# Moving a 32-byte tile from below the weight slots to above them, in a hybrid decoder layer

## The chip, the cores and the metric

The kernel runs on one core of a Trainium2 chip. The metric is the device time of one execution in microseconds (us). A core has five engines that run side by side and meet at semaphores: TensorE (PE in the profile; its weight loads are listed apart as PEld), VectorE (DVE), ScalarE (ACT), GpSimd (POOL) and SyncE (SP), which here only issues DMAs. Tiles lie in the on-chip memory SBUF, 128 partitions wide; an address below is a byte offset inside each partition.

## The reference, cut to what matters

```python
h = rms_norm(x, mix_norm)                       # x: 1024 tokens x 1024
z = h @ w_in                                    # columns: GLA q,k,v,r, low rank | SWA q,k,v
o_gla = gla_chunked(...)                        # gated linear attention, 4 heads, then rms norm and SiLU gate
o_swa = swa_sink_attention(...)                 # window 128, 8 query heads, 2 key heads, ALiBi, sinks
x = x + concat([o_gla, o_swa]) @ w_out
h2 = rms_norm(x, ffn_norm)
u = causal_dwconv(h2 @ w_up, conv_w, conv_b)    # 1024 x 5632, three taps
a, b = split(u, 2)
return x + (silu(a) * b) @ w_down               # 2816 x 1024
```

Everything is float32 and there is one layer.

## The kernel before, in words

Each large product is made in float32r from a high and a low part of both factors (`split`, L88 to L95: `hi` is a rounded copy, `lo` the rest), in three matmuls: high x high, high x low, low x high (`PASSES`). A matmul has a stationary operand (128 x 128, `lhsT`) and a moving one (`rhs`, mostly 128 x 512), and every one has its own weight load.

- Tokens are tiles of 128. The input projections (`dense`, L317, and `unit_q_part`, L707) run over eight token tiles and eight row blocks: `lhsT` is a piece of the normalized, transposed input in `big`, `rhs` a weight block. PSUM names are `dq`, `dk`, `dv`, `dg`, `dr` for the parts of `z` and `do` for the output projection. `dk` has 272 columns, the others 512.
- Between them run the two attentions, with small matmuls and transposes.
- The up-projection (`product`, L834) uses Strassen's seven products for each of 22 chunks of columns: `lhsT` is a weight block (`A11`, `A12`, `A22` or a sum `S1` to `S4` of blocks), `rhs` four token tiles at once, 128 x 4 x 128, from `big` or from `ex` (sums of token blocks). Each product is 12 matmuls. PSUM names are `gb` for most of chunk 0 and `fb` for the others; `fb` also serves the last rows.
- The down-projection (`down_pair`, L1015) uses seven products for each pair of chunks, 10 pairs, in groups of six matmuls that stand between the up products: `lhsT` is `dg` (activations), `rhs` is `dw` (weights), PSUM `dn_P`. The last two chunks are done in `last_row` (L1044, PSUM `dl` and `fb`) from `dnw` and `g`.

Order of the work: the first part is pinned in a list (`FIRST`); after it each step has a due time (`at`, `at_us`) and the program is written out in the order of those times.

Memory: pools on the left grow up from the bottom, pools with `side="right"` grow down from the top. The first pool on the right is `wa` (`w_keep`), nine slots of 2 x 512 floats, 4096 bytes each. `slot_tile` hands out slots, `w_tile` walks through them by `SLOTS`. They hold all the split weights of the projections but seven blocks of `dk`, the up operands, both operands of the down products and the raw rows of `w_down`. Under it lies `idp` with `ident` (512 bytes, the identity for transposes) and `mhalf` (8 floats, 32 bytes), filled with -0.5 and read by GpSimd as the exponent in `rms_scale` and `norm1_stat`. `idp` is closed by `open_ff`, before the tiles of the convolution are opened there. The addresses of the program before:

| tile | address | remainder by 64 |
|---|---|---|
| `big` (activations, high and low) | 1152 | 0; all pieces are 512 bytes apart |
| raw tiles, `kw` (seven blocks of `dk`), `ex` (token sums) | 67392 and on, 160320, 112448 | 0 |
| `A11w` and `A12w` of chunk 1, in the pool `pn` | 178240, 182336 | 0 |
| `w9`, one late slot: block 0 of the second half of `w_out` | 187840 | 0 |
| `ident` | 191936 | 0 |
| `mhalf` | 192448 | 0 |
| nine slots | 192480 + 4096 s, s = 0 to 8 | 32 |
| end of the usable memory | 229344 | 32 |

```python
    w_keep = ctx.enter_context(tc.tile_pool(name="wa", bufs=1, side="right"))
    idp = swp.enter_context(tc.tile_pool(name="idp", bufs=1, side="right"))
    def slot_tile(slot, name, dt=F32R):
        return w_keep.tile([P, 2, 512], dt, tag=f"w{slot}", name=name, bufs=1)
    # product (L834): w from a slot, or from pn for A11 and A12 of chunk 1
    pe.matmul(pb, lhsT=w[:, ra, k, :], rhs=b_operand(bn, k, rb), ...)
    # dense (L317): ws[k] from a slot, from kw or w9
    pe.matmul(pb[:, :n], lhsT=big[:, t, k, ra, :], rhs=ws[k][:, rb, :n], ...)
    # down_pair (L1015): both from slots
    pe.matmul(pb[:, i], lhsT=g[:, ra, c:c + P], rhs=w[:, rb, :], ...)
```

Of the kernel before, what the change touches and what calls it, by code (L numbers as in the profile page):

```python
# [9 lines left out]
F32 = mybir.dt.float32  # L10
# [7 lines left out]
P = 128  # L18
# [16 lines left out]
def hymba_layer_kernel(ctx, tc, x, mix_norm, w_in, w_alpha2, b_alpha, gla_norm,  # L35
# [33 lines left out]
    def raw_tile(name):  # L69
        return base.tile([P, 1024], F32, tag="raw", name=name, bufs=RAW_BUFS)  # L70

    w_keep = ctx.enter_context(tc.tile_pool(name="wa", bufs=1, side="right"))
    w_late = {}
    swp = ExitStack()
    idp = swp.enter_context(tc.tile_pool(name="idp", bufs=1, side="right"))
# [39 lines left out]
    upper = gl.tile([P, P], F32, name="upper")  # L115
    amask = upper.bitcast(I32)
    ind = gl.tile([P, 2], F32R, name="ind")
    mhalf = idp.tile([P, 8], F32, name="mhalf")
    pool.memset(mhalf, -0.5)

    ones_r = gl.tile([P, P], F32R, name="ones_r")
# [1182 lines left out]
```

## Time and profile before

| | |
|---|---|
| median of 3 runs | 1054.98 us (1054.74 to 1055.16) |
| profiled execution, span from first to last instruction | 1053.6 us |
| median less span | 1.4 us |
| matmuls, busy time of TensorE | 4976, 1046.6 us |
| weight loads | 4976, 851.0 us |
| VectorE, ScalarE, GpSimd busy | 799.4, 480.2, 617.7 us |
| DMA moved | 67.13 MB, mean 64 GB/s |

The page gives of the profiled execution its span; the time around it is not listed there, so the median is set against the span. Busy times of TensorE add up overlapping, pipelined matmuls, with modelled ends; how fast it goes is read from the starts of successive matmuls. In the chain that ended last each row is a stretch: start in us, length in us, what ran, and how many instructions.

### The profile page before, as it was taken

The numbers are of one execution on the slowest core, as the hardware profiler recorded it, in microseconds if no ns is written. First come the engines' busy times: TensorE is split into PE (matmuls) and PEld (weight loads), VectorE is DVE, ScalarE is ACT, GpSimd is POOL, SyncE is SP. The second block draws the span as 40 slices with busy tenths as digits, with TensorE's granted clock in tenths as the row PEclk, the third lists the DMA queues.
The fourth block names the chain that finished last, engine by engine and source line by source line (L and its number), as shares of the span: only waits on it lengthen the run. The fifth ranks groups of instructions, "written<-read, shape, count | busy, mean of one in ns | idle before, by whom it ended". The sixth has DMA issues, their size and how long they took to land.

```text
span 1053.6 us, 13921 instructions
## 1 busy us (share of the span) xinstructions
PE 1046.6 (99%) x4976; PEld 851.0 (81%) x4976; DVE 799.4 (76%) x1332; ACT 480.2 (46%) x988; POOL 617.7 (59%) x510
## 2 busy tenths in 40 slices
PE   9999999999999999999999999999999999999998
PEld 6898877888888888888888888888888888888887
DVE  6776667754131699887979898897979798897976
ACT  5527655444340346554444445444444444444441
POOL 4592132325450205867868687877778687978750
PEclk9999999999999999999999999999999999999999
DMA  6152113002044202112121111212121211121104
GB/s 213 61 152 61 44 49 92 21 1 81 1 122 159 60 1 80 40 41 81 40 80 34 49 51 49 60 61 61 40 80 40 61 40 45 56 61 60 41 20 160
DMA packets 67502, 67.13 MB, mean 64 GB/s; under 512 B 4648, under 2 KB 52201, under 8 KB 67434
## 3 DMA queue, kind: packets, MB, share of 16 engines
q1 hardware_dynamic: 63448, 61.27, 18.7%
q10 hardware_dynamic: 3986, 4.99, 2.0%
q8 instruction: 39, 0.64, 0.2%
q14 instruction: 29, 0.24, 0.1%
HBM read 57.33 MB, written 4.19 MB: 58 GB/s over the span
## 4 chain that ended last, share of the span: by engine, by line
PE 97%; DMA 1%; DVE 1%; ACT 0%; issue 0%; POOL 0%; DVEq 0%; ACTq 0%; SPq 0%
PE fb L834 39%; PE dn_P L1015 18%; PE do L317 9%; PE dr L317 4%; PE dv L317 4%; PE dg L317 4%; PE dq L317 3%; PE dk L317 2%; PE gb L834 2%; PE dq L707 1%; PE pv L490 1%; PE dl L1044 1%; PE fb L1044 1%; PE go L600 1%; PE ga L591 1%; PE sc L443 1%
## 5 line engine op out<-in xcount | busy, mean ns | idle before, releaser
L1019 DVE TENSOR_TENSOR acc<-acc,dn_P 128x1024 f32<-128x1024 f32 x140 | 169.8, 1214 | 65.6 <-PE dn_P L1015 65.5
L1015 PE MATMUL dn_P<-dw,dg 128*128 128x512 f32 x840 | 215.8, 392 | 0.0
L1015 PEld LDWEIGHTS dn_P<-dw,dg 128*128 128x128 f32 x840 | 157.7, 188 | 37.1
L317 PE MATMUL do<-wow,big 128*128 128x512 f32 x384 | 92.9, 398 | 0.0
L317 PEld LDWEIGHTS do<-wow,big 128*128 128x128 f32 x384 | 71.1, 188 | 16.3
L95 POOL TENSOR_TENSOR dw<-dn,dw 128x512 fp32r<-128x512 f32 x50 | 69.1, 1381 | 25.3 <-PE dn_P L1015 19.5
L886 ACT COPY ca<-fb 128x512 f32<-128x512 f32 x62 | 36.3, 585 | 72.8 <-PE fb L834 72.7
L834 PE MATMUL fb<-big,A11w 128*128 128x512 f32 x252 | 63.0, 396 | 0.0
L834 PE MATMUL fb<-big,S4w 128*128 128x512 f32 x252 | 62.9, 396 | 0.0
L834 PE MATMUL fb<-big,S1w 128*128 128x512 f32 x252 | 62.9, 396 | 0.0
L834 PE MATMUL fb<-ex,S2w 128*128 128x512 f32 x252 | 62.8, 396 | 0.0
L834 PE MATMUL fb<-ex,S3w 128*128 128x512 f32 x252 | 62.8, 396 | 0.0
L841 DVE SCALAR_TENSOR_TENSOR ua<-fb,cc,ua 128x511 f32<-128x511 f32 x84 | 62.2, 740 | 0.5 <-ACT ua L846 0.3
L834 PE MATMUL fb<-big,A12w 128*128 128x512 f32 x252 | 62.5, 396 | 0.0
L834 PE MATMUL fb<-ex,A22w 128*128 128x512 f32 x252 | 62.5, 397 | 0.0
L834 PEld LDWEIGHTS fb<-big,A11w 128*128 128x128 f32 x252 | 47.4, 188 | 11.6
L834 PEld LDWEIGHTS fb<-big,S1w 128*128 128x128 f32 x252 | 47.4, 188 | 11.6
L834 PEld LDWEIGHTS fb<-big,S4w 128*128 128x128 f32 x252 | 47.4, 188 | 11.6
L834 PEld LDWEIGHTS fb<-ex,S2w 128*128 128x128 f32 x252 | 47.4, 188 | 11.4
L834 PEld LDWEIGHTS fb<-ex,A22w 128*128 128x128 f32 x252 | 47.4, 188 | 11.4
L834 PEld LDWEIGHTS fb<-ex,S3w 128*128 128x128 f32 x252 | 47.4, 188 | 11.4
L834 PEld LDWEIGHTS fb<-big,A12w 128*128 128x128 f32 x252 | 47.3, 188 | 11.1
(432 smaller groups left out, 2402.7 us busy)
## 6 DMA issues: line engine op xcount, KB each, us to landing
up<-in_w_up_dram SPq DMA_DIRECT2D x44, 512.0 KB, 3.9
dn<-in_w_down_dram SPq DMA_DIRECT2D x22, 512.0 KB, 3.5
acc<-in_x_dram SPq DMA_DIRECT2D x8, 512.0 KB, 6.9
out_dram<-acc SPq DMA_DIRECT2D x15, 256.0 KB, 2.0
xt<-in_x_dram SPq DMA_DIRECT2D x7, 512.0 KB, 3.4
vraw<-in_w_in_dram SPq DMA_DIRECT2D x4, 512.0 KB, 3.7
graw<-in_w_in_dram SPq DMA_DIRECT2D x4, 512.0 KB, 3.6
qt<-qt ACTq DMA_DIRECT2D x16, 128.0 KB, 2.2
```

The lines of the kernel that those rows point to most:

```text
L95: (eng or pool).tensor_sub(lo, src, hi.bitcast(F32))
L317: pe.matmul(pb[:, :n], lhsT=big[:, t, k, ra, :], rhs=ws[k][:, rb, :n], start=(k == 0 and i == 0), stop=(k == KD - 1 and i == 2))
L443: pe.matmul(pbs[-1][:, j % 2, :], lhsT=ql[:, g, qc], rhs=kt[:, g, kc], start=False, stop=True)
L490: pe.matmul(pbs[i][HALF[g]], lhsT=vv[rows, t - 1 + b, HALF[g]], rhs=rhs[rows, :, HALF[i]], start=start, stop=stop)
L591: pe.matmul(pb[:, pr * 256:(pr + 1) * 256], lhsT=gqt[t][:, pr, :], rhs=qbd[t % 2][:, pr], start=(pr == 0), stop=(pr == 1))
L600: pe.matmul(pb[:, h * P:(h + 1) * P], lhsT=asb[:, h, :], rhs=v[:, h * P:(h + 1) * P], start=(h == 0), stop=(t == 0 and h == 3))
L834: pe.matmul(pb, lhsT=w[:, ra, k, :], rhs=b_operand(bn, k, rb), start=(onto is None and i == 0), stop=(i == 11), skip_group_check=onto is n ...
L841: dve.scalar_tensor_tensor(dst, src, w, dst, op0=ALU.mult, op1=ALU.add)
L886: act.copy(dst, pb)
L1015: pe.matmul(pb[:, i], lhsT=g[:, ra, c:c + P], rhs=w[:, rb, :], start=(onto is None and n == 0), stop=(n == 2), skip_group_check=onto is no ...
L1019: dve.tensor_add(acc, acc, pb)
L1044: pe.matmul(pb[:, c0:c1], lhsT=g[:, ra, (t % 4) * P:(t % 4 + 1) * P], rhs=w[:, rb, c0:c1], start=(ch == NCH - 2 and i == 0), stop=(ch == N ...
```

## The change

`mhalf` gets a pool of its own, `edge`, which is opened first on the right side and stays open to the end. It lies at 229312, the slots begin at 192448 + 4096 s, 32 bytes lower, where `mhalf` was, and `ident` and everything below it keep their addresses. All nine slots then begin at multiples of 64.

```diff
@@ -69,6 +69,8 @@
     def raw_tile(name):
         return base.tile([P, 1024], F32, tag="raw", name=name, bufs=RAW_BUFS)
 
+    edge = ctx.enter_context(tc.tile_pool(name="edge", bufs=1, side="right"))
+    mhalf = edge.tile([P, 8], F32, name="mhalf")
     w_keep = ctx.enter_context(tc.tile_pool(name="wa", bufs=1, side="right"))
     w_late = {}
     swp = ExitStack()
@@ -115,7 +117,6 @@
     upper = gl.tile([P, P], F32, name="upper")
     amask = upper.bitcast(I32)
     ind = gl.tile([P, 2], F32R, name="ind")
-    mhalf = idp.tile([P, 8], F32, name="mhalf")
     pool.memset(mhalf, -0.5)
 
     ones_r = gl.tile([P, P], F32R, name="ones_r")
```

## The prediction

> **What bounds the kernel now.** I read the page first: busy times, slices, the chain that ended last.
>
> ```profile
> span 1053.6 us, 13921 instructions
> PE 1046.6 (99%) x4976; PEld 851.0 (81%) x4976; DVE 799.4 (76%) x1332; ACT 480.2 (46%) x988; POOL 617.7 (59%) x510
> PEclk9999999999999999999999999999999999999999
> PE 97%; DMA 1%; DVE 1%; ACT 0%; issue 0%; POOL 0%; DVEq 0%; ACTq 0%; SPq 0%
> ```
>
> TensorE is busy nearly always, at the full granted clock, and 97% of the chain is its own matmuls one behind another. The list of what TensorE waited for (engine, line, releaser: us in total, times, longest) is as short as this:
>
> ```profile
> PE warm L1085 <- DVE warm L124: 1.7, 1, 1.7
> PE dg L317 <- ACT vg L720: 0.9, 1, 0.9
> PE dq L707 <- POOL qw L295: 0.3, 1, 0.3
> PE gb L834 <- ACT big L255: 0.2, 1, 0.2
> PE dq L707 <- DVE big L259: 0.2, 1, 0.2
> ```
>
> 3.3 us in all. So the time is set by the distance from one matmul's start to the next, times the count, and nothing else is worth much. A matmul's listed duration does not show that distance, since matmuls overlap (392 ns listed, for one every 230). The chain in order of time does: start, us, what, and how many. The sum by line of the whole chain, then the stretch in which the up-projection begins, then three other stretches:
>
> ```profile
> by line: PE fb L834 39.2%; PE dn_P L1015 18.4%; PE do L317 8.5%; PE dr L317 4.3%; PE dv L317 3.7%; PE dg L317 3.7%; PE dq L317 2.7%; PE dk L317 2.3%; PE gb L834 1.9%; PE dq L707 1.3%; PE pv L490 1.2%; PE dl L1044 1.0%; PE fb L1044 1.0%; PE
> ...
> 312.97 47.83 PE do L317 x205
> 390.38 6.75 PE do L317 x29
> ...
> 403.14 2.81 PE gb L834 x12
> 405.95 2.30 PE fb L834 x10
> ...
> 410.29 2.75 PE fb L834 x12
> ...
> 441.11 14.06 PE fb L834 x60
> ...
> 464.01 1.36 PE dn_P L1015 x6
> ...
> 468.19 1.39 PE dn_P L1015 x6
> ...
> 1036.46 2.72 PE fb L1044 x12
> ```
>
> Divide, and set each beside the addresses in the map above. All these matmuls have the same shape, 128x128 stationary against 512 moving columns:
> - Rows of `do` (L317): 47.83 / 205 = 233.3 ns. Moving operand in a slot (32 past a multiple of 64), stationary in `big` (a multiple of 64).
> - Up products: 14.06 / 60 = 234.3, 2.81 / 12 = 234.2. Stationary in a slot, moving in `big` or `ex`. Again one of each kind.
> - The last rows (L1044): 2.72 / 12 = 226.7. Both operands in slots: both 32 past.
> - Down products (L1015), both in slots: 1.36 / 6 = 226.7 in one row, 1.39 / 6 = 231.7 in another; over all, 18.4% of 1053.6 us / 840 = 230.8. They are slower just behind an up product.
> - The two up products of chunk 1 whose weights do not lie in a slot but in the pool `pn`, at multiples of 64:
>
> ```profile
> 405.79 2.46 PE L834 MATMUL fb<-big,A11w 128*128 128x512 f32 x10
> ...
> 410.04 2.99 PE L834 MATMUL fb<-big,A12w 128*128 128x512 f32 x12
> ```
>
> These timeline rows name them in the chain: 2.30 / 10 = 230.0 (A11w, just behind an ordinary product) and 2.75 / 12 = 229.2 (A12w). The same function with the same moving tile, 3 us earlier (`gb`, weights in a slot), needs 234.2. So pairs of operands that lie alike modulo 64 run at 226.7 to 230 ns, and unlike pairs at 233.3 to 234.3. The trace does not say why; the difference itself is what I price.
>
> **The change part by part.** It adds and removes no instruction, semaphore or DMA. `edge` takes the top 32 bytes, the nine slots go 32 bytes down to 192448 + 4096 s, and `ident` and everything below keep their addresses, because the 32 bytes that leave `idp` are those the slots now take. After it every large matmul has both operands at multiples of 64. The counts:
>
> ```profile
> L834 PE MATMUL fb<-big,A11w 128*128 128x512 f32 x252 | 63.0, 396 | 0.0
> ...
> L834 PE MATMUL fb<-ex,A22w 128*128 128x512 f32 x252 | 62.5, 397 | 0.0
> ...
> L834 PE MATMUL gb<-ex,A22w 128*128 128x512 f32 x12 | 3.0, 395 | 0.0
> ...
> L1015 PE MATMUL dn_P<-dw,dg 128*128 128x512 f32 x840 | 215.8, 392 | 0.0
> L317 PE MATMUL do<-wow,big 128*128 128x512 f32 x384 | 92.9, 398 | 0.0
> L317 PE MATMUL dg<-gw,big 128*128 128x512 f32 x192 | 47.9, 403 | 0.9 <-ACT vg L720 0.9
> ...
> L317 PE MATMUL dv<-vw,big 128*128 128x512 f32 x192 | 47.5, 400 | 0.0
> L317 PE MATMUL dq<-qw,big 128*128 128x512 f32 x120 | 29.3, 399 | 0.0
> ```
>
> 1. **Up products.** Seven operands with 252 fb and 12 gb rows each, 7 x 264 = 1848, less the 24 that are alike already: 1824. Pace now (39.2% of 1053.6) / 1764 = 234.1 ns. Ends: 234.1 (nothing gained) and 226.7 (as the last rows): 0 to 1824 x 7.4 = 13.5 us. I take 229.2, the A12w row, since it is the same function with the same three-dimensional moving tile: 1824 x 4.9 = 8.9 us.
> 2. **Input and output projections** with 512 columns at L317: 384 + 3 x 192 (`dg`, `dr`, `dv`) + 120 = 1080, less 24 on the late slot `w9`, which lies at a multiple of 64 already: 1056. The first 72 of `dq` (L707) wait for operands in the start and are given nothing. Pace 233.3; ends 0 and (233.3 - 226.7) x 1056 = 7.0 us. The nearest row is a thin one: the last 29 matmuls of `do`, three of them on `w9`, took 6.75 us where 29 x 233.3 is 6.77, so some 5 ns for each of the three, with 10 ns of rounding over all three. A mark that small can't settle it; I take 3 ns, a little under half of the span: 3.2 us.
> 3. **Down products**: 840. Both operands move together and stay alike, so their own best, 226.7, should stay; what can go is the slow start behind an unlike up product. Ends: 840 x (230.8 - 226.7) = 3.4 us gained, and 840 x (234.1 - 230.8) = 2.8 us lost if it is the odd 32 that suits a pair. I take half of the gain, 1.7 us, since the six-matmul rows above stand at both values.
> 4. **Last rows** at L1044: at 226.7 already, nothing. The **24 of `dk`** whose moving operand is a slot (`kw7`, 272 columns): at 7.4 ns 0.2 us at most; nothing taken.
> 5. **The other engines** that write and read slots. ScalarE and GpSimd take the same time for 512 columns wherever the tile lies:
>
> ```profile
> L92 ACT CAST A12w<-up x22: 617/622/625, 351.7 to 994.9; 128x512 fp32r<-128x512 f32 x22
> L92 ACT CAST big<-qo x8: 615/621/622, 255.2 to 306.1; 128x512 fp32r<-128x512 f32 x8
> ...
> L95 POOL TENSOR_TENSOR A12w<-up,A12w 128x512 fp32r<-128x512 f32 x20 | 25.9, 1294 | 0.0
> ...
> L789 POOL TENSOR_TENSOR up<-up 128x512 f32<-128x512 f32 x21 | 27.2, 1295 | 1.6
> ...
> dn<-in_w_down_dram SPq DMA_DIRECT2D x22, 512.0 KB, 3.5
> up<-in_w_up_dram SPq DMA_DIRECT2D x44, 512.0 KB, 3.9
> ```
>
> 622 against 621 ns (a slot, `big`); 1294 against 1295 (a slot, raw tiles at multiples of 64); a load into slots lands in 3.5 us, one into raw tiles in 3.9. Nothing. `mhalf` keeps its readers; the late `ff` pool no longer follows its release, which is worth nothing while TensorE waits for nobody.
>
> Sum: 8.9 + 3.2 + 1.7 = 13.8 us. Against the profiled execution 1053.6 - 13.8 = 1039.8; the median of 1054.98 stands 1.4 us above that span, so **1041.2 us**. A faster TensorE must still be fed:
>
> ```profile
> 70.00:316.00 246.00, 244.96 (x1453) 203.40 (x1453) 141.48 (x408) 121.15 (x367) 92.38 (x91) 1.00 0.21 56
> 460.00:1020.00 560.00, 560.00 (x2406) 451.77 (x2405) 487.74 (x601) 261.22 (x443) 431.06 (x315) 1.00 0.18 53
> ```
>
> In the long stretch from 460 to 1020 us (columns TensorE, weight loads, VectorE, ScalarE, GpSimd) VectorE works 487.7 of 560 us and GpSimd 431.1. If the stretch shrinks to about 550, VectorE is at 89%: the next to be late, not yet the bound.
>
> The Trainium skill, in "SBUF — State Buffer", section "Specifications (TRN2)", gives SBUF 16-byte cachelines and a penalty for each cross to a new one. Multiples of 32 and of 64 both begin such a line, so by that page nothing would change and the time would stay 1055.0. The A12w row, 229.2 against 234.2, disagrees with it as far as it goes, but 24 matmuls at one place are few, which is why the next rival keeps its share.
>
> **The rivals.**
> - *Nothing changes (same).* The quicker pace of `A11w` and `A12w` of chunk 1 belongs to something other than the position modulo 64: their place in another part of memory, or the distance to `big`. For it: only 24 matmuls, and the `w9` tile as moving operand shows next to nothing. Against it: the last rows and half of the down rows are quick too, at quite other places. 1055.0, up to 0.5 us off. This is also what the 16-byte rule gives. 14%.
> - *Slower: an equal pair is quick because both lie 32 past.* Then up and projection matmuls gain nothing, and the down products fall to 234.1: +2.8 us, and the last rows (8 rows x 2 halves x 2 chunks x 3 passes, and 6 for the split last half: 102 matmuls) lose up to 102 x 7.4 = 0.8 us: 1058.5. It decides as soon as steps 1 and 2 bring less than the 2.8 us. Against it stand the two products at multiples of 64 with 229 to 230. 6%.
> - *Only the up products gain* (steps 2 and 3 zero): 1054.98 - 8.9 = 1046.1. Or VectorE, at 87%, takes back part of the gain in its full slices; with a third of 13.8 lost, 1045.8. Faster still. 30%.
> - *All pairs reach 226.7*: 13.5 + 7.0 + 3.4 = 23.9 us, 1031.1. 10%.
> - *The forecast itself*, 1036 to 1044: 40%.
>
> **How the numbers follow.** 0.2%, 2.1 us, is about what a measurement of this kernel tells from no change. Faster: 40 + 30 + 10 = 80%; same 14%, slower 6%. The forecast is the likeliest case, 1041.2. Its kind (faster) lies in 1031 to 1050. To leave out no more than two in ten, the case of no change must be in: 1031 to 1056, which leaves the slower case and the tails.
>
> **What would show it.** Step 1: chain rows of twelve `fb` L834 at 2.75 instead of 2.81, and the share of `fb` at 1764 x 229.2 = 404 us instead of 413. Step 2: the long `do` run near 230 ns for each, instead of 233.3. Step 3: `dn_P` rows of six at 1.36 throughout; the last rows unchanged at 2.72 for twelve. Step 5: durations of the casts and subtractions unchanged, waits of TensorE still under some 5 us. The prediction is wrong if the `fb` rows keep 2.81 (no change), if `dn_P` goes to 1.40 (slower), or if the list of TensorE's waits grows by VectorE entries.

## The result, and the profile after

The changed kernel takes 1047.99 us (1047.32 to 1048.54) against 1054.86 before: ratio 0.9936, 95% interval 0.9922 to 0.995. Faster by 6.9 us, where 13.8 were forecast; inside the range, half the size.

The page after, then the list of what TensorE waited for:

```profile
span 1045.6 us, 13921 instructions
...
PE 1038.6 (99%) x4976; PEld 849.3 (81%) x4976; DVE 799.0 (76%) x1332; ACT 480.5 (46%) x988; POOL 618.4 (59%) x510
...
PEclk9999999999999999999999999999999999999999
```

```profile
PE warm L1086 <- DVE warm L125: 1.7, 1, 1.7
PE dg L318 <- ACT vg L721: 1.0, 1, 1.0
PE dq L708 <- POOL qw L296: 0.3, 1, 0.3
...
```

The same instructions, the same waits and the same granted clock, and a span shorter by 8.0 us. The chain in order of time shows which matmuls follow one another faster (start, us, what, how many; line numbers are one higher than before):

```profile
by line: PE fb L835 39.3%; PE dn_P L1016 18.5%; PE do L318 8.4%; PE dg L318 4.2%; PE dr L318 4.2%; PE dv L318 3.7%; PE dq L318 2.6%; PE dk L318 2.3%; PE gb L835 1.9%; PE dq L708 1.3%; PE pv L491 1.2%; PE dl L1045 1.0%; PE fb L1045 1.0%; PE 
...
309.05 46.94 PE do L318 x205
...
400.67 2.33 PE fb L835 x10
...
405.03 2.75 PE fb L835 x12
...
701.59 2.80 PE fb L835 x12
704.38 1.38 PE dn_P L1016 x6
705.76 2.79 PE fb L835 x12
708.56 1.38 PE dn_P L1016 x6
...
1028.41 2.72 PE fb L1045 x12
```

- Projections: 46.94 / 205 = 229.0 ns, 4.3 less. On 1056 matmuls 4.6 us.
- Up products: 39.3% of 1045.6 / 1764 = 232.9, 1.2 less; 2.80 / 12 = 233.3 on `big` (701.59), 2.79 / 12 = 232.5 on `ex` (705.76). On 1824 matmuls 2.2 us.
- Down products: a row of 1.38 / 6 = 230.0, against a mean of 230.8 before: 0.8 x 840 = 0.7 us.
- The last rows stand at 226.7, as before. A12w of chunk 1 too, 2.75 / 12 = 229.2, while A11w (400.67) went from 230.0 to 233, though neither its address nor that of `big` had moved.

4.6 + 2.2 + 0.7 = 7.5 us by these rows. Added up over the starts of all matmuls in the two traces it is 7.0: 4.1 in the projections (their runs of 24 go from 5.60 to 5.51 us, 3.8 ns each), 2.3 in the up products, 0.6 in the down products. Another 0.7 of the 8.0 us lies in the start of the execution, where a row of eight `dq` begins at 12.87 instead of 13.58 us; in the other versions below it begins between 12.79 and 13.80, so this is not put down to the change. After the change, then, the operands of all up products lay alike modulo 64, and yet all but A12w of chunk 1 kept a slow pace. That is the question for the experiments.

### The profile page after: what moved, and what is told of

The parts are those of the page before. It is cut to its first block, busy times and chain, and to the rows that moved or that the text cites. A ratio compares the mean times of both kernels' runs of the same rounds, so it can differ in the third digit from the quotient of the medians.

```text
span 1045.6 us, 13921 instructions
## 1 busy us (share of the span) xinstructions
PE 1038.6 (99%) x4976; PEld 849.3 (81%) x4976; DVE 799.0 (76%) x1332; ACT 480.5 (46%) x988; POOL 618.4 (59%) x510
## 4 chain that ended last, share of the span: by engine, by line
PE 98%; DVE 1%; ACT 0%; DMA 0%; POOL 0%; issue 0%; ACTq 0%; SPq 0%
PE fb L835 39%; PE dn_P L1016 18%; PE do L318 8%; PE dg L318 4%; PE dr L318 4%; PE dv L318 4%; PE dq L318 3%; PE dk L318 2%; PE gb L835 2%; PE dq L708 1%; PE pv L491 1%; PE dl L1045 1%; PE fb L1045 1%; PE go L601 1%; PE ga L592 1%; PE sc L443 1%
```

## The experiments

**Pairs by themselves.** The body of the kernel becomes loops of the two forms of matmul over 112 pairs of start addresses, with a rest between pairs (the edit in short):

```diff
+ for kind, b, s in COMBOS:              # b, s: offsets of activations and slots, bytes
+     pb = psum tile of one bank, read by VectorE before the next pair
+     form d: matmul(pb, lhsT=act4[:, t, k, ra, :], rhs=slots[s + k, rb, 0:512])   x96
+     form u: matmul(pb, lhsT=slots[s, ra, k], rhs=act4[:, 0:4, k, rb, :])         x48
```

> This kernel leaves the whole layer out. It runs only matmuls of the two shapes of the large products, in float32r, 96 (form d, as in the projections: stationary from the activations, moving contiguous from a slot) or 48 (form u, as in the up products: stationary from a slot, moving in four pieces of 128 from the activations) for each of 112 pairs of start residues modulo 512; before each pair TensorE waits for the last one's result to be read, so every pair starts from rest. The theory of the prediction, that what counts is whether both operands lie alike modulo 64, expects 226.7 to 229.2 ns from start to start for every alike pair and 233.3 to 234.3 for every unlike one, whatever the distance. The rival, that the distance modulo 512 counts beside it, expects the alike pairs to differ among themselves: about 233 for form u at (activations 128, slot 448) and (320, 448), as the up products of the changed kernel show, 229 at (128, 64), and 229 for form d at (128, 448). The second rival, that the pace is a rhythm which a run of matmuls keeps from the state in which it started, expects all alike pairs of form u to run at about 229 here, since each starts from rest as A12w of chunk 1 does, (128, 448) too.

The timeline of TensorE (start, us, the run, the idle time before it). A name gives form, activations and slot, each by a letter for the start modulo 512 in steps of 32 (a 0, b 32, c 64, e 128, g 192, k 320, o 448, p 480):

```profile
939.89 22.56 PE L63 MATMUL d_ea<-slots,big 128*128 128x512 f32 x96 [0.25 <-DVE sink L68]
962.71 22.75 PE L63 MATMUL d_eb<-slots,big 128*128 128x512 f32 x96 [0.26 <-DVE sink L68]
985.72 22.67 PE L63 MATMUL d_ec<-slots,big 128*128 128x512 f32 x96 [0.25 <-DVE sink L68]
1008.64 22.06 PE L63 MATMUL d_ee<-slots,big 128*128 128x512 f32 x96 [0.25 <-DVE sink L68]
1030.95 22.26 PE L63 MATMUL d_eg<-slots,big 128*128 128x512 f32 x96 [0.26 <-DVE sink L68]
1053.46 22.66 PE L63 MATMUL d_ek<-slots,big 128*128 128x512 f32 x96 [0.26 <-DVE sink L68]
1076.38 22.27 PE L63 MATMUL d_eo<-slots,big 128*128 128x512 f32 x96 [0.26 <-DVE sink L68]
...
1793.02 11.26 PE L67 MATMUL u_ec<-big,slots 128*128 128x512 f32 x48 [0.25 <-DVE sink L68]
1804.54 11.18 PE L67 MATMUL u_ee<-big,slots 128*128 128x512 f32 x48 [0.26 <-DVE sink L68]
...
1839.22 11.47 PE L67 MATMUL u_eo<-big,slots 128*128 128x512 f32 x48 [0.25 <-DVE sink L68]
1850.94 11.51 PE L67 MATMUL u_ep<-big,slots 128*128 128x512 f32 x48 [0.26 <-DVE sink L68]
```

Subtract the start of the stationary operand from that of the moving one, modulo 256. Form d, moving in the slot: `ee` 0, 22.06 us for 96; `eg` and `eo` (448 - 128 = 320) both 64, 22.26 and 22.27; `ea` 128, 22.56; `ec` and `ek` 192, 22.67 and 22.66; `eb` an odd multiple of 32, 22.75. Form u, moving in the activations: `ee` 0, 11.18 for 48; `ec` 64, 11.26; `eo` (128 - 448, so 192) 11.47; `ep` odd, 11.51. The steps between the starts of the later matmuls of each run, once it has settled, are

| moving minus stationary, modulo 256 | ns from start to start |
|---|---|
| 0 | 226.7 |
| 64 | 228.9 |
| 128 | 232.1 to 233.5 |
| 192 | 233.3 |
| odd multiples of 32 | 233.3 to 234.3 |

and they come out the same for both forms and for all bases tried, except at 128, where form u settles at 232.1 to 232.3 for four pairs and at 233.5 for five. This difference, called the distance from here on, counts, with its sign; being alike modulo 64 does not suffice. In the changed kernel the projections had 64, the up products on `big` 192, those on `ex` 128; A11w and A12w of chunk 1 alone had 64. The rival of a rhythm kept from the start falls here: (128, 448) of form u runs at the slow pace from rest too.

**Both odd, and parted.** Two controls that need no new addresses for the slots:

```diff
+    base.tile([P, 8], F32, name="pad")          # x1: in the kernel before; x2: in the changed one
     big = base.tile([P, NT, KD, 2, P], F32R, name="big")
```

> The kernel before with 32 bytes put under the activations, so that big, ex and the raw tiles lie 32 past a multiple of 64 as the slots do: every pair alike, at the odd place. Alike theory: as the changed kernel or better, 1042 to 1050, dense runs at 229, up products 233 or less, down products 227 to 231. If a multiple of 64 is good in itself for an operand, slower than the changed kernel: dense runs stay at 233.3 and up products at 234, 1055 or more.

> The changed kernel with the same 32 bytes under the activations: slots at multiples of 64, activations 32 past. Unlike pairs again, the other way round. Alike theory: back at 1054 to 1056, dense runs at 233.3, up products at 234. If a multiple of 64 is good in itself, half of the gain stays (one operand of two is still at one): about 1051.

Both odd: 1047.99 us, ratio to before 0.9932 (0.9916 to 0.9949): the time of the changed kernel, with `big` and the slots 32 past a multiple of 64. Parted: 1052.75, ratio 0.9981 (0.9971 to 0.999). The longest `do` runs of the two, the chain of each:

```profile
309.83 46.97 PE do L318 x205
```

```profile
311.66 47.83 PE do L319 x205
```

229.1 and 233.3 ns. So the gain needs no multiple of 64, and slots at one do nothing for the projections by themselves. Parted lies outside both of its forecasts, 1054 to 1056 and 1051: its projections are back, but it stays 2.2 us below the kernel before. Its four products on `big` went from distance 160 to 224, 234.3 to 233.3 ns by the runs of pairs, and its three on `ex` from 96 to 160, the other way; that would leave some 0.2 us. Over the starts of the two traces the up products gain 1.1, so the paces of long runs don't carry over to odd distances in this alternation; the rest is not explained. Both odd has exactly the distances of the changed kernel, 64, 192 and 128; the two theories of the distance and of alike pairs agree here, which the next run parts.

**Same remainder by 64, other distance.** `cc`, 704 bytes, goes below `big`, which moves to 1856; the pad of the runs above is gone again:

```diff
+    cc = base.tile([P, 4, 44], F32, name="cc")
     big = base.tile([P, NT, KD, 2, P], F32R, name="big")
...
-    cc = base.tile([P, 4, 44], F32, name="cc")
```

> The changed kernel with cc, 704 bytes, put below the activations instead of above: big goes from 1152 to 1856, all else stays. All pairs remain alike modulo 64. Alike theory: nothing changes, 1048. Distance theory: in the projections moving minus stationary goes from 64 to 128 modulo 256, dense runs from 229.1 to about 232.4, some 3.5 us more; the up products on big go from 192 to 128, from 233.3 to between 232 and 233.3, 0 to 1.3 us less: 1050 to 1052.

1050.04 us, ratio 0.9953 (0.9936 to 0.9969): 2 us slower than the changed kernel, although every pair is still alike modulo 64. The `do` run of its chain:

```profile
311.50 47.64 PE do L319 x205
```

232.4 ns, the pace of distance 128. The theory of the prediction is gone.

**What a run keeps from the one before, fewer columns, finer steps.** Again matmuls alone, some without a rest between pieces (the edit in short; the numbers in brackets are starts of activations and slot).

```diff
+ ("from_unlike", [u(128,480) x12, u(128,64) x12, ...]), ("from_three", [u(128,448) x12, u(128,64) x12, ...])
+ ("mix_after", 4 x [u(128,448) x12, both in slots x6]), ("mix_zero", 4 x [u(128,128) x12, both in slots x6])
+ half: form d with 256 columns, most: 384, short: 128; eq 0, sixtyfour 64, opposite 128, three 192, odd 32
+ sixteen: form d, distances of odd multiples of 16
```

> This kernel leaves the whole layer out and runs only matmuls, in float32r. The theory now: the steady pace of 512-column matmuls follows the distance moving start minus stationary start modulo 256 (0: 226.7 ns, 64: 228.9, 128: about 232, 192: 233.3, odd multiples of 32: 233.3 to 234.3), and a run keeps the pace of what went before for some matmuls. First part, form u without a rest between pieces: (128, 64) of 12 behind (128, 480) goes down to 229 within a few matmuls, as A11w of chunk 1 did before; behind (128, 448) it stays at 233.3 for all 12, as it did after, and if that is a state which holds, for the 72 of the longer piece too. Distance 0 behind 233.3 falls to 226.7 in about six matmuls. The rival, that the pair alone sets the pace, expects 229 in both from the second matmul on. The mix of 12 up and 6 down matmuls at (128, 448): 233.3 and about 230, at distance 0 all 226.7. Second part, form d with fewer columns: if the cost hangs on the weight load, the surplus of distance 192 over 0 is the same 6.7 ns at 384 and 256 columns; if it hangs on the columns streamed, it shrinks with them to 5 and 3.3. Third part, distances of odd multiples of 16: with banks of 32 bytes they go as their neighbours, 233 to 234; with banks of 16, otherwise.

```profile
43.49 2.92 PE L71 MATMUL from_unlike_b<-big,slots 128*128 128x512 f32 x12
46.25 2.98 PE L71 MATMUL from_unlike_c<-big,slots 128*128 128x512 f32 x12
...
68.88 2.92 PE L71 MATMUL from_three_b<-big,slots 128*128 128x512 f32 x12
71.63 2.96 PE L71 MATMUL from_three_c<-big,slots 128*128 128x512 f32 x12
...
144.74 1.54 PE L75 MATMUL mix_after_f<-slots 128*128 128x512 f32 x6
146.12 2.96 PE L71 MATMUL mix_after_g<-big,slots 128*128 128x512 f32 x12
...
161.72 1.52 PE L75 MATMUL mix_zero_f<-slots 128*128 128x512 f32 x6
163.08 2.88 PE L71 MATMUL mix_zero_g<-big,slots 128*128 128x512 f32 x12
165.80 1.52 PE L75 MATMUL mix_zero_h<-slots 128*128 128x512 f32 x6
...
196.72 6.01 PE L67 MATMUL half_eq_a<-slots,big 128*128 128x256 f32 x48 [0.25 <-DVE sink L77]
202.98 5.71 PE L67 MATMUL half_sixtyfour_a<-slots,big 128*128 128x256 f32 x48 [0.26 <-DVE sink L77]
...
215.16 5.73 PE L67 MATMUL half_three_a<-slots,big 128*128 128x256 f32 x48 [0.26 <-DVE sink L77]
```

From start to start of successive pieces: (128, 64) takes 2.76 us behind an odd pair and 2.75 behind distance 192, 229 to 230 ns each. So here the pair sets the pace at once, and my idea of a held state is wrong in this form. It is not refuted for the changed kernel. The twelve matmuls at (128, 448) here go in steps that alternate between 231 and 236 ns; those ahead of A11w of chunk 1 go 233, 233, 234, and A11w goes on in these steps. Its ten matmuls take 2.33 us behind distance 192, and 2.30 and 2.29 in the two versions below in which the products ahead lie at distance 0 and 64, though A11w and `big` are where they were. So what ran before matters there; why is open. A few matmuls do go into the settling: six of distance 0 behind twelve of distance 192 take 1.38 us (144.74 to 146.12), as `dn_P` in the changed kernel, and 1.36 among their like. With 256 columns the order turns round: 48 at distance 0 take 6.01 us, at 64 and 192 5.71 and 5.73, some 6 ns a matmul the other way. Neither theory on the columns foresaw that. Nor did they foresee 384 columns, where the settled pace is 173.3 ns at 0 and at 64, 176.1 at 128 and 174.5 at 192; with 128 columns it is 111.7 at every distance tried. Odd multiples of 16 lay between 231.1 and 236.7 ns, not always with their neighbours.

**Distance 0 to `big`**, with 64 bytes more above the slots:

```diff
     mhalf = edge.tile([P, 8], F32, name="mhalf")
+    edge.tile([P, 16], F32, name="pad")
```

> The changed kernel with 64 bytes more above the slots, which begin at 192384: distance 0 modulo 256 to big, and moving minus stationary 192 for the products on ex. Distance theory: dense runs at 226.7 (2.5 us less), the four up products on big at 226.7 to 229 (4.5 to 7 us less, since twelve matmuls behind slower ones take some time to fall), the three on ex at 233.3 (up to 0.4 us more), down products 0 to 2 us less: 1037 to 1042. Alike theory: 1048.

1040.16 us, ratio 0.9856 (0.9841 to 0.987). The chain:

```profile
309.71 46.51 PE do L319 x205
...
702.48 2.80 PE fb L836 x12
705.28 1.38 PE dn_P L1017 x6
706.66 2.72 PE fb L836 x12
709.38 1.36 PE dn_P L1017 x6
```

The projections went from 229.0 to 226.9 ns, the products on `big` from 233.3 to 226.7 (2.72 / 12, behind 706.66), those on `ex`, now at distance 192, go from 232.5 to 233.3 (2.80 / 12). A down group takes 1.38 behind `ex` and 1.36 behind `big`: what it loses comes from the piece ahead of it. By these paces 1032 products on `big` (four of the seven, less 24) bring 6.6 x 1032 = 6.8 us, the projections 2.1 x 1056 = 2.2, and 792 products on `ex` lose 0.8 x 792 = 0.6: 8.4 us, where 7.8 were measured, and the down products, which gain too, are not in this sum. The pads move other tiles on that side too, which I did not follow.

**The slots at 192320**, with `big` and `ex` where they were: the distances of projections and up products on `big` change places.

```diff
+    edge.tile([P, 16], F32, name="pad")
...
-        e = psb[key, ch] = fin["ff"].tile([P, 2], F32, tag="e", name=f"{key}_{ch}", bufs=2)
+        e = psb[key, ch] = edge.tile([P, 2], F32, tag="e", name=f"{key}_{ch}", bufs=2)
```

> The changed kernel with 128 bytes more above the slots (64 of padding and the two tiles of edge columns), big and ex where they were: the slots start at 192320. Moving minus stationary modulo 256 is then 64 for the up products on big, the distance that A12w of chunk 1 had, 0 for those on ex, and 192 for the projections: the reverse of the changed kernel, in which the projections had 64 and the up products on big 192. Distance theory with its sign: products on big at about 229, products on ex at 226.7 to 228, projections back at 233.3; 1056 x 4.4 and 792 x 6 less, 1056 x 4.2 more, down products up to 2 us less: 1039 to 1044. If the distance counted without its sign, both would keep what 64 and 192 share, and up products and projections would stand at one pace: dense runs stay at 229 and the time falls to 1036 to 1039. Alike theory: 1048.

1045.3 us, ratio 0.991 (0.9894 to 0.9927): 1.3 us above the range of 1039 to 1044. The chain:

```profile
312.96 47.84 PE do L319 x205
...
703.65 2.76 PE fb L836 x12
706.41 1.39 PE dn_P L1017 x6
707.79 2.74 PE fb L836 x12
710.54 1.36 PE dn_P L1017 x6
```

The sign of each move is as the table has it: the projections are back at 233.4, `big` (distance 64) is at 230.0, `ex` (distance 0) at 228.3. But in this alternation neither reaches the pace it has by itself, 228.9 and 226.7. On 1032 products of `big` that is 1.1 us and on 792 of `ex` 1.3 us: the table is for long runs, and each change of distance between pieces costs some 10 to 30 ns here. That much I had left out.

**Distance 0 for all**, the last diff and that of `cc` together:

> cc below the activations and 128 bytes more above the slots (64 of padding, and the two small tiles of edge columns moved there), so that big, ex, the nine slots, the late slot and A11w and A12w of chunk 1 all start at 64 modulo 256. Distance theory: every large matmul at 226.7: against the changed kernel 1848 x 6.4 for the up products, 1056 x 2.4 for the projections, 840 x 3.6 for the down products, 17.4 us less, 1030.6, between 1029 and 1034. Alike theory: 1048. If VectorE becomes the bound in the long stretch, 1035 to 1040 with new waits of TensorE for it.

1033.15 us, ratio 0.9793 (0.9779 to 0.9808): the best version, 14.8 us below the changed kernel. Its chain, and the new row in the list of what TensorE waited for:

```profile
309.29 46.50 PE do L320 x205
...
703.33 2.72 PE fb L836 x12
706.04 1.36 PE dn_P L1017 x6
```

```profile
PE fb L836 <- DVE ua L843: 0.3, 1, 0.3
```

46.50 / 205 = 226.8, 2.72 / 12 and 1.36 / 6 = 226.7: one pace, and nothing lost between pieces of one distance. The stretch from 450 to 1000 us, the columns as in the prediction:

```profile
450.00:1000.00 550.00, 550.00 (x2427) 455.28 (x2426) 489.20 (x604) 262.40 (x445) 432.62 (x316) 1.00 0.18 55
```

VectorE works 489.2 of 550 us, 89%, and for the first time TensorE waits for it behind `ua`, once, for 0.3 us. It is the next to be late, not yet the bound.

## Why the prediction was wrong in its size

The sign held and so did the frame: no instruction changed, TensorE waited for the same things, its pace changed, and the time lies inside the range. The gain was half of the forecast, and the step that failed is the first, in its mechanism and not in its size alone: the prediction held pairs that lie alike modulo 64 to be quick, and the run with `big` at 1856 has only such pairs and is 2 us slower than the changed kernel.

1. **Up products: 8.9 us forecast, 2.2 measured.** The rows of twelve were to go to 2.75 us and stand at 2.80 and 2.79. I took 229.2 ns from A12w of chunk 1, because it was the same function with the same moving tile and both operands at multiples of 64. What made it quick was another relation of the two addresses. `big` lies at 128 modulo 256 and A12w at 64: distance 64. The change brought the slots to 192, and with it distance 192 on `big` and 128 on `ex`, whose settled paces are 233.3 and 232.1 to 233.5. Both numbers stood in my address map; only the remainder by 64 was read from it. The rival "nothing changes" named the doubt, "the distance to `big`", and took it for a reason why nothing at all would change. None of the rows I read stood at 128 or 192, where the change puts all up products but those 24, so none of them could price it.
2. **Projections: 3.2 us forecast, 4.6 measured by the long row, 4.1 over all starts.** They did get distance 64 and went to 229.0. That was luck of the addresses: at distance 128, alike modulo 64 too, the long row takes 232.4 each. The mark for that was there: the three matmuls on `w9`, at 187840, had distance 64 too, and their 5 ns, which I marked down to 3, were near the 4.3 measured.
3. **Down products: 1.7 us forecast, 0.7 measured.** "They are slower just behind an up product" was right, and half of the gain was to go with the unlike neighbour; but the neighbour stayed slow. In the best version all six take 1.36, and over the starts of all 840 that is 2.9 us less than before (193.5 to 190.6), most of the 3.4 at the upper end of this step.
4. **Last rows** unchanged at 2.72 for twelve, as forecast.
5. **The other engines** unchanged, and TensorE waits for nothing new:

```profile
L790 POOL TENSOR_TENSOR up<-up 128x512 f32<-128x512 f32 x21 | 27.2, 1294 | 1.6
...
dn<-in_w_down_dram SPq DMA_DIRECT2D x22, 512.0 KB, 3.5
```

Of the rivals, "slower: quick because both lie 32 past" fell with the projections: both operands at multiples of 64, and 4.3 ns less. "All pairs reach 226.7", 1031.1 us, priced what the best version gives, 1033.15; it needed distances that the change doesn't make. "Only the up products gain", 1046.1, lies nearest to the measured time for a wrong reason: the projections gained more than the up products.

The Trainium skill, "TensorE: Matmul & The Clock Gate", section "Step-by-step: what each phase is for", says that TensorE has two independent read ports into SBUF, one for the moving operand and one for weight loads, and that loading the next weights takes no bandwidth from the running matmul. Read as a rule for the pace, it would have the distance count for nothing; 226.7 against 233.3 ns for the same shape disagrees with that reading. Nor does the 16-byte line that the prediction weighed, from the Trainium skill's "SBUF — State Buffer", section "Specifications (TRN2)", tell 0 from 64 or 192: all are multiples of 16. What makes the distance count, no run here shows.

Open stay: the mechanism; what A11w of chunk 1, at distance 64, keeps from the products at 192 ahead of it in the changed kernel; and the order at 256 columns. The pieces of an operand lie multiples of 512 bytes apart, so a moving operand has the same distance to its own stationary operand and to the next one of its run: no run here tells which of the two counts.

## What to carry to other kernels

Where a kernel is bound by the pace of its matmuls, read the time from start to start from the chain (length over count) for each pair of operands, and write beside it the difference of the two start addresses, not each address's own alignment. For 512 columns of fp32r it paid to bring moving and stationary operand to the same remainder by 256 bytes: 2.1% here, by 64 bytes of padding and moving `mhalf`, `cc` and the two tiles of edge columns. When a price is borrowed from a row, that row must share every address relation which the change will make; and for other column counts the pace has to be measured anew.

## What the runs showed of the hardware

- The pace of a matmul with its own weight load, 512 columns, goes from 226.7 to 234.3 ns with the distance of its operands modulo 256, in multiples of 32, at the full granted clock.
- With 256 columns distances 64 and 192 are quicker than 0: 5.71 and 5.73 us against 6.01 for 48.
- A piece behind one of another distance often pays some 10 to 30 ns once: 1.38 or 1.39 against 1.36 us for six. A11w of chunk 1 kept 233 ns for all ten matmuls behind distance 192, where its own pace is 229.
